# A decoder step on one core: the block inverse widened from 16 to 32, the last output blocks divided 400 and 144, and two products over zeros at the start

## The chip, the cores and the metric

The kernel runs on one core of one Trainium2 chip. Its engines are TensorE (PE, matrix products; PEld is its weight load), VectorE (DVE), ScalarE (ACT), GpSimd (POOL) and SyncE (SP, which issues most of the DMAs). The metric is the time of one execution on the device in microseconds; the time of a kernel is the median of its runs.

## The reference: what is computed

One step of a decoder with one layer, for 512 prompt tokens and 8 sample sequences of 4 tokens, 1024 channels wide. All data is float32. Cut to what matters:

```python
h = rms_norm(x, pre_mix_g)
proj = h @ w_in                               # 1024 x 7424
A = conv_branch(proj[:, :2048])               # GLU, causal conv of width 31, LayerNorm, silu, @ w_conv_out
r, k, v, decay, a, g = ...                    # from proj, with token shift; 16 heads of 64
def step(s, inp):                             # the RWKV-7 recurrence, per head, s is 64 x 64
    r_t, w_t, k_t, v_t, kk_t, a_t = inp
    sk = einsum('bhvk,bhk->bhv', s, kk_t)
    s = s * w_t - sk * (kk_t * a_t) + v_t * k_t
    return s, einsum('bhvk,bhk->bhv', s, r_t)
B = ((group_norm(y) + bonus) * g) @ w_rwkv_out
m = (sigmoid(gA) * A + sigmoid(gB) * B) @ w_out
x = x + rms_norm(m, post_mix_g)
f = square(relu(rms_norm(x, pre_ffn_g) @ w_ff_up)) @ w_ff_down
x = x + rms_norm(f, post_ffn_g)
```

Outputs are the new x and the conv, shift and recurrence states.

## The kernel before

**Layout.** Channels lie on the 128 partitions (8 tiles of 128), tokens on columns: 544 columns, 552 where the 8 shift rows ride along. They are worked in two parts, S1 (276 and 276) or S2 (272 and 272).

**Products.** A weight block of 128 output channels (1024 x 128) is loaded by SP into `raw` (`wraw`, two buffers) and divided into a high part and the remainder, both of type fp32r: `whi` by a cast on ACT or POOL (L140), `wlo` by a subtraction on DVE (L141), two buffers each. The activations are divided likewise (`xh`, `xl`, L173 and L174). A block's product over one part is then 3 matmuls for each of the 8 input tiles (L152 in `part_steps`: whi with xh, whi with xl, wlo with xh). A plain f32 matmul appears in the trace as two records.

**Stages.** x is loaded and normalised (the squares come from ACT at L260, the mean from f32 matmuls with the constant `avg`, L261, one for each of 8 tiles and 2 parts). Then come the blocks of w_in, and between them the recurrence, by pairs of heads (8 pairs, `p`). For a pair the 512 prompt tokens are divided in 8 chunks of 64. Inside a chunk the recurrence is a linear system with a strictly triangular 64 x 64 matrix for each head: its Gram blocks come from PE (L553), are masked into `NQ` and `nd`, and `inverse` replaces the chunk's triangular matrix by the inverse. `chain(p)` then goes through the chunks one after the other (L672 to L687) with `NQ`. Behind it stand `sample` for the sample tokens, the group norm and the output `o`, which goes through DRAM (`o_dr`) to the product with w_rwkv_out. Conv steps (L292, one DVE instruction for each of 31 taps and 8 tiles) fill DVE meanwhile. After the recurrence follow the gate blocks, w_rwkv_out, the LayerNorm of the conv branch (sums L881, variance sum L169), w_conv_out, w_out, and the two halves of the feed-forward part.

**The inverse.** Each chunk's 64 x 64 matrix holds two 32 x 32 diagonal blocks for each of two heads. `nd` with the diagonal blocks is transposed on DVE into `nw` (L588), so that a row of each block lies along the free axis. Fifteen steps of forward substitution (a product, L597, and a subtraction, L599, each on both 16-halves of each block at once) invert the 16 x 16 diagonal blocks in `R`. Two transposes (L602, L604) give `td` and `rd`; copies on ACT (L609) and POOL (L610) set them into the zeroed 64-wide tiles `DT64` and `D64`. What lies outside the 16-blocks, `NQ` under `maskD`, is then brought in by four products, each 8 f32 matmuls, one a chunk (L616): MT = N D, and three times x = D - MT x, the last of which writes `NQ` (L633), the two before it `nw` (L630).

**The end.** The last two blocks of w_ff_down (`last`, 48 matmuls a part) are done part by part: both blocks for the first 272 columns, then both for the second. Their evacuation (L1028) adds the first half's result, `acc_sq` squares it on ACT (L880) and sums it (L881); `rstd` takes the mean over channels on PE (L169) and its inverse root; then for each of 8 tiles two DVE instructions (L1059, L1060) and a store of that tile and part (L1061).

**What sets the order.** A scheduler of the tile framework sets each engine's order from the program, priorities and estimates; the generators' `yield` statements say how the steps of pairs are woven with blocks of projections.

## Time and profile before

| | before |
|---|---|
| median of 3 runs | 1300.46 us (1299.64 to 1304.72) |
| profiled execution, its time | 1299.37 us |
| its span, first to last instruction | 1297.6 us |
| mean granted clock of PE | 0.989 |
| DVE busy | 819.9 us in 1545 instructions |
| ACT busy | 652.0 us in 1563 instructions |
| PE waits for the first product's DT (L609) | 7.8 us, 7 times |

A row of a group reads: line, engine, operation, output from inputs, shape, count, then busy time in us, mean of one in ns, and the idle time of that engine just before them with what ended it. A row of a timeline begins with start and duration in us; the bracket at its end holds the idle time before it. The span is the base of all positions in time. Matmuls follow each other in a pipeline, so what one costs is the distance of starts, not its own duration.

### The profile page before, as it was taken

How to read it: one execution, taken by the hardware profiler on the slowest of the kernel's cores; microseconds unless marked ns; L12 is line 12 of the kernel's file. 1: busy time of each engine (PE TensorE's matmuls, PEld its weight loads, DVE VectorE, ACT ScalarE, POOL GpSimd, SP SyncE). 2: the span in 40 equal slices, each digit the busy share in tenths (PEclk: the TensorE clock that was granted, in tenths of full speed). 3: DMA queues.
4: the chain of work that ended last, by engine and by line, in shares of the span. 5: the costliest groups of instructions: out<-in, count | busy, mean ns of one | idle time of the engine just before them, and what ended most of it. 6: DMA issues, size and time to landing. Idle time of an engine off the chain costs nothing. (4 is left out here: it accounts for less than half of the span.)

```text
span 1297.6 us, 23134 instructions
## 1 busy us (share of the span) xinstructions
PE 1238.4 (95%) x9154; PEld 1162.8 (90%) x9154; DVE 819.9 (63%) x1545; ACT 652.0 (50%) x1563; POOL 198.0 (15%) x286
## 2 busy tenths in 40 slices
PE   7989999999999999999999999999999999999995
PEld 6978888887978888787889999999999999999995
DVE  6889889855888898887677465658432122333345
ACT  7453747575563747538244382356554223554231
POOL 2224232221323233132201100000000000000000
PEclk9989999999999999999999999999999999999998
DMA  6313121120202121131115642361122332232332
GB/s 202 104 33 109 33 82 34 49 69 19 84 33 96 34 81 33 33 95 42 67 48 195 220 167 92 110 209 50 34 82 82 98 86 94 82 97 75 90 98 70
DMA packets 45181, 110.60 MB, mean 85 GB/s; under 512 B 7056, under 2 KB 16528, under 8 KB 45072
## 3 DMA queue, kind: packets, MB, share of 16 engines
q1 hardware_dynamic: 41344, 104.33, 25.6%
q10 hardware_dynamic: 3728, 4.79, 1.1%
q8 instruction: 72, 1.18, 0.4%
q14 instruction: 37, 0.30, 0.1%
HBM read 94.79 MB, written 14.32 MB: 84 GB/s over the span
## 5 line engine op out<-in xcount | busy, mean ns | idle before, releaser
L152 PE MATMUL lin<-xh,whi 128*128 128x272 f32 (+1 forms) x2096 | 616.2, 294 | 4.1 <-DVE r L394 2.0
L152 PE MATMUL lin<-xh,wlo 128*128 128x272 f32 (+1 forms) x2096 | 615.6, 294 | 0.6 <-DVE wlo L141 0.6
L152 PE MATMUL lin<-xl,whi 128*128 128x272 f32 (+1 forms) x2096 | 614.2, 293 | 0.4 <-DVE xl L174 0.2
L152 PEld LDWEIGHTS lin<-xh,whi 128*128 128x128 f32 x2096 | 397.0, 190 | 7.2 <-issue 2.9
L152 PEld LDWEIGHTS lin<-xl,whi 128*128 128x128 f32 x2096 | 396.5, 189 | 3.7 <-issue 1.4
L152 PEld LDWEIGHTS lin<-xh,wlo 128*128 128x128 f32 x2096 | 396.6, 189 | 3.1 <-issue 1.4
L141 DVE TENSOR_TENSOR wlo<-raw,whi 128x1024 fp32r<-128x1024 f32 x131 | 160.7, 1227 | 197.8 <-ACT whi L140 175.7
L292 DVE SCALAR_TENSOR_TENSOR c<-u,cw,c 128x512 f32<-128x512 f32 x240 | 188.0, 783 | 5.7 <-DVE c L292 1.2
L140 ACT CAST whi<-raw 128x1024 fp32r<-128x1024 f32 x76 | 79.7, 1049 | 122.7 <-PE lin L152 119.2
L140 POOL CAST whi<-raw 128x1024 fp32r<-128x1024 f32 x55 | 65.4, 1189 | 319.0 <-PE lin L152 182.9
L152 PE MATMUL lin<-xh,wl 128*128 128x272 f32 x240 | 69.4, 289 | 0.0
L152 PE MATMUL lin<-xl,wh 128*128 128x272 f32 x240 | 69.3, 289 | 0.0
L152 PE MATMUL lin<-xh,wh 128*128 128x272 f32 x240 | 69.2, 288 | 0.0
L1001 DVE TENSOR_TENSOR xl<-ff,xh 128x272 fp32r<-128x272 f32 x64 | 28.3, 442 | 55.9 <-ACT ff L1000 55.9
L687 ACT ACTIVATE SV<-ch,pc 64x64 f32<-64x64 f32 x128 | 39.6, 309 | 19.2 <-PE ch L683 17.8
L228 ACT ACT_TABLE_LOAD x37 | 47.5, 1283 | 1.8 <-PEq L1124 1.2
L152 PEld LDWEIGHTS lin<-xh,wl 128*128 128x128 f32 x240 | 45.2, 188 | 0.1
L152 PEld LDWEIGHTS lin<-xh,wh 128*128 128x128 f32 x240 | 45.2, 188 | 0.1
L152 PEld LDWEIGHTS lin<-xl,wh 128*128 128x128 f32 x240 | 45.1, 188 | 0.1
L681 ACT ACTIVATE SV<-ch 64x64 f32<-64x64 f32 x128 | 27.9, 218 | 33.6 <-PE ch L679 31.6
L760 POOL TENSOR_SCALAR st<-st,epS 128x64 f32<-128x64 f32 x64 | 39.9, 673 | 7.9 <-DVE rt L597 7.9
L998 ACT ACTIVATE ff<-lin 128x272 f32<-128x272 f32 x64 | 25.3, 395 | 29.6 <-PE lin L152 29.5
(274 smaller groups left out, 1830.4 us busy)
## 6 DMA issues: line engine op xcount, KB each, us to landing
raw<-win SPq DMA_DIRECT2D x58, 512.0 KB, 3.7
raw<-wup SPq DMA_DIRECT2D x32, 512.0 KB, 3.6
raw<-wdn SPq DMA_DIRECT2D x32, 512.0 KB, 3.6
g_dr<-g ACTq DMA_DIRECT2D x16, 272.0 KB, 2.9
raw<-wro SPq DMA_DIRECT2D x8, 512.0 KB, 3.7
raw<-wco SPq DMA_DIRECT2D x8, 512.0 KB, 3.6
raw<-wo SPq DMA_DIRECT2D x8, 512.0 KB, 3.6
x<-xT SPq DMA_DIRECT2D x8, 276.0 KB, 4.7
```

The source lines that it names most:

```text
L140: upper(hi, r)
L141: tt(out=lo, in0=r, in1=hi.bitcast(F32), op=SUB)
L152: nc.tensor.matmul(ps, a, b[:, o:o + m], start=k == 0 and i == 0, stop=k == n - 1 and i == 2)
L228: lastact[0] = nc.scalar.preload_act_table_set(name)
L292: stt(out=c[:, 0:T], in0=u[:, t:t + T], scalar=w[:, t:t + 1], in1=c[:, 0:T], op0=MULT, op1=ADD)
L681: nc.scalar.mul(SV[H[i], c, i, :], ch[H[i], 2, B[i]], -1.0)
L687: nc.scalar.mul(SV[H[i], c + 1, i, :], ch[H[i], 1, B[i]], pc[H[i], c:c + 1])
L760: nc.gpsimd.tensor_scalar(st[:, b, :], st[:, b, :], f["epS"][:, b:b + 1], None, MULT)
L998: act(t[:, q], ps, AF.Relu)
L1001: tt(out=lo[:, q], in0=t[:, q], in1=hi[:, q].bitcast(F32), op=SUB)
```

## The change

Three parts. (1) The forward substitution runs 31 steps over whole 32 x 32 blocks instead of 15 over 16 x 16 halves; `maskD` leaves out the whole 32-blocks, and of the four products two remain: MT = N D and one x = D - MT D, which writes `NQ`. (2) The last two down blocks are divided in 400 and 144 columns (S3) instead of two times 272, with the norm, the final operations and the stores. (3) A tile `warm` of 128 x 512 zeros is set on DVE, and two f32 matmuls with `avg` run over it before the statistics of x.

```diff
--- before.py
+++ after.py
@@ -28,6 +28,7 @@
 RMS_EPS, LN_EPS, GN_EPS, KK_EPS = 1e-6, 1e-5, 64e-5, 1e-24
 CDEC = math.exp(-0.5)
 NFP, NFIRST, NPG, UB = 44, 6, 2, 2
+NWARM = 2
 KEPT = 2
 CP, HP, HN = 300, 900, 130
 PUMP, WB, WL, WR = 5, 2, 2, 2
@@ -38,6 +39,7 @@
 
 S1 = ((0, 276), (276, 276))
 S2 = ((0, 272), (272, 272))
+S3 = ((0, 400), (400, 144))
 
 VECS = [("pre_mix_g", 8), ("post_mix_g", 8), ("pre_ffn_g", 8), ("post_ffn_g", 8), ("conv_b", 8),
         ("conv_ln_g", 8), ("conv_ln_b", 8), ("decay_base", 8), ("iclr_base", 8), ("k_k", 8),
@@ -249,6 +251,12 @@
             ready.append(wsplit(raws[-1]))
         avg = p0.tile([128, 128], F32, name="avg")
         nc.vector.memset(avg, 1.0 / D)
+
+        warm = p0.tile([128, 512], F32, name="warm")
+        nc.vector.memset(warm, 0.0)
+        wps = q0.tile([128, 512], F32, name="warmps")
+        for _ in range(NWARM):
+            nc.tensor.matmul(wps, avg, warm, start=True, stop=True)
         rs, rt = (p0.tile([128, N1], F32, name=n) for n in ("rs", "rt"))
         hfs = [p0.tile([128, N1], F32, name=f"hf{k}") for k in range(KT)]
         with start:
@@ -353,16 +361,13 @@
         nc.gpsimd.memset(maskD, 0.0)
         maskP = p1.tile([128, 2, 64], F32, name="maskP")
         nc.gpsimd.memset(maskP, 0.0)
-        first16 = p1.tile([128, 1], F32, name="first16")
-        nc.vector.tensor_reduce(out=first16, in_=con("bmask")[:, 0:4], op=ADD, axis=mybir.AxisListType.X)
         for i in range(2):
             q = slice(64 * i, 64 * i + 64)
             nc.scalar.copy(maskD[q, :, i, :], mask[q].rearrange("p (a t) -> p a t", a=2))
             nc.scalar.copy(maskP[64 * i:64 * i + 32, i, :], maskS[64 * i:64 * i + 32])
             for g in range(2):
                 r, o = slice(64 * i + 32 * g, 64 * i + 32 * g + 32), 32 * g
-                nc.gpsimd.memset(maskD[r, 0, i, o:o + 16], 0.0)
-                nc.scalar.copy(maskD[r, 0, i, o + 16:o + 32], first16[r].to_broadcast([32, 16]))
+                nc.gpsimd.memset(maskD[r, 0, i, o:o + 32], 0.0)
         zar = p1.tile([128, NB, 16], F32, name="zar")
         nc.gpsimd.memset(zar, 0.0)
         zbk = p1.tile([128, 2, 64], F32, name="zbk")
@@ -588,14 +593,12 @@
             nc.vector.transpose(nt.rearrange("p s t -> p t s"),
                                 nd.rearrange("p c t -> p t c").unsqueeze(3).to_broadcast([128, 32, NC, 4]))
             yield DVE
-            half = lambda t, d, o, n: bass.AP(tensor=t.tensor, offset=t.offset + o, ap=[t.ap[0], [d, 2], *n])
-            for s in range(15):
-                nj, n = s // 4 + 1, 15 - s
-                tmp = p1.tile([128, 64], F32, name="rt")
-                tv = tmp[:, 0:2 * nj * n].rearrange("p (a j t) -> p a j t", a=2, j=nj)
-                rv = half(R, 144, s + 1, [[32, nj], [1, n]])
-                tt(out=tv, in0=half(R, 144, s, [[32, nj], [0, n]]),
-                   in1=half(nt, 528, 33 * s + 1, [[0, nj], [1, n]]), op=MULT)
+            for s in range(31):
+                nj, n = s // 4 + 1, 31 - s
+                tv = p1.tile([128, 80], F32, name="rt")[:, 0:nj * n].rearrange("p (j t) -> p j t", j=nj)
+                rv = R[:, 0:nj, s + 1:32]
+                tt(out=tv, in0=R[:, 0:nj, s:s + 1].to_broadcast([128, nj, n]),
+                   in1=nt[:, s:s + 1, s + 1:32].to_broadcast([128, nj, n]), op=MULT)
                 tt(out=rv, in0=rv, in1=tv, op=SUB)
                 yield DVE
             td = p1.tile([128, NC, 32], F32, name="td", tag="nd")
@@ -623,16 +626,10 @@
                 for i in range(2):
                     nc.scalar.copy(MT[H[i], :, i, :], ps[H[i]])
             yield from product(lambda c: NQ[:, c, 0], DT64, to_m)
-            x = D64
-            for it in range(3):
-                def to_x(ps):
-                    if it < 2:
-                        tt(out=xn, in0=D64, in1=ps, op=SUB)
-                    else:
-                        for i in range(2):
-                            tt(out=NQ[H[i], :, 0, i, :], in0=D64[H[i]], in1=ps[H[i]], op=SUB)
-                yield from product(lambda c: MT[:, c], x, to_x)
-                x = xn
+            def to_x(ps):
+                for i in range(2):
+                    tt(out=NQ[H[i], :, 0, i, :], in0=D64[H[i]], in1=ps[H[i]], op=SUB)
+            yield from product(lambda c: MT[:, c], D64, to_x)
 
         def tokens(p):
 
@@ -880,9 +877,9 @@
             act(sq[:, q], src[:, q], AF.Square)
             tt(out=acc[:, q], in0=acc[:, q], in1=sq[:, q], op=ADD)
 
-    def rstd(rs, acc, eps, s):
+    def rstd(rs, acc, eps, s, split=S2):
         t = temp("rt")
-        f32sum(con("avg"), acc, S2[s:s + 1],
+        f32sum(con("avg"), acc, split[s:s + 1],
                lambda _, ps, o, m: rsqrt(rs[:, o:o + m], ps, eps, t[:, o:o + m]), **aux)
 
     def rstd_sum(rs, src, eps, s):
@@ -1049,11 +1046,11 @@
                 linear(w, fhl, S2, down(j))
 
     last = [(j, wload(wdn[j, 2], pg) + wload(wdn[j, 3], pg)) for j in (KT - 2, KT - 1)]
-    for s in range(2):
-        q = HALF[s]
+    for s, (o, m) in enumerate(S3):
+        q = slice(o, o + m)
         for j, w in last:
-            part_mm(w, fhl, s, *S2[s], down(j), pl2, "lin")
-        rstd(rs, acc, rms_eps, s)
+            part_mm(w, fhl, s, o, m, down(j), pl2, "lin")
+        rstd(rs, acc, rms_eps, s, S3)
         for j in range(KT):
             f = part[j][:, q]
             stt(out=f, in0=f, scalar=nvec("post_ffn_g", j), in1=rs[:, q], op0=MULT, op1=MULT)
```

In the changed kernel L154 is L152 of before, L143 is L141, L171 is L169, L300 is L292, L600 and L602 are the substitution's L597 and L599, L878 is L881, L1025 is L1028, L1056 and L1057 are L1059 and L1060.

DVE in the inverse of pair 0, between the transposes into `nw` and `td`. Before (`rt` and `R` are the substitution, `c` a conv step):

```order
L597 TENSOR_TENSOR rt<-R,nw 128x36
L292 SCALAR_TENSOR_TENSOR c<-u,cw,c 128x512
L599 TENSOR_TENSOR R<-R,rt 128x2x2x9
L289 TENSOR_SCALAR c<-u,cw,vt 128x512
L597 TENSOR_TENSOR rt<-R,nw 128x32
L292 SCALAR_TENSOR_TENSOR c<-u,cw,c 128x512
L599 TENSOR_TENSOR R<-R,rt 128x2x2x8
```

And now, where `wlo` is a weight's remainder and `k` a part of the next pair's projections:

```order
L600 TENSOR_TENSOR rt<-R,nw 128x63
L300 SCALAR_TENSOR_TENSOR c<-u,cw,c 128x512
L602 TENSOR_TENSOR R<-R,rt 128x3x21
L143 TENSOR_TENSOR wlo<-raw,whi 128x1024
L600 TENSOR_TENSOR rt<-R,nw 128x60
L392 SCALAR_TENSOR_TENSOR k<-lin,omu,k 128x276
L602 TENSOR_TENSOR R<-R,rt 128x3x20
L300 SCALAR_TENSOR_TENSOR c<-u,cw,c 128x512
L600 TENSOR_TENSOR rt<-R,nw 128x76
L300 SCALAR_TENSOR_TENSOR c<-u,cw,c 128x512
L602 TENSOR_TENSOR R<-R,rt 128x4x19
```

An operation of the substitution still alternates with one other instruction, but there are 62 instead of 30 of them: 127 instructions stand between the two transposes, 61 before.

PE behind the recurrence, where `aux` from `acc` is the variance sum of the conv LayerNorm. Before, it stands inside a gate block (`lin_7677`):

```order
L152 MATMUL lin_7677<-xh_91,wlo_7623 128x272
L152 MATMUL lin_7677<-xh_93,whi_7622 128x272
L152 MATMUL lin_7677<-xl_94,whi_7622 128x272
L152 MATMUL lin_7677<-xh_93,wlo_7623 128x272
L169 MATMUL aux_8550<-acc_8517,cs_74 128x272
L169 MATMUL aux_8559<-acc_8517,cs_74 128x272
L152 MATMUL lin_7677<-xh_95,whi_7622 128x272
L152 MATMUL lin_7677<-xl_96,whi_7622 128x272
```

Now it stands among the first products with w_rwkv_out (`lin_8224`, `lin_8250`, `lin_8285`; `xh_8168` to `xl_8199` are parts of `o`):

```order
L154 MATMUL lin_8250<-xl_8193,whi_8220 128x272
L154 MATMUL lin_8250<-xh_8192,wlo_8221 128x272
L154 MATMUL lin_8285<-xh_8168,wlo_8282 128x272
L154 MATMUL lin_8285<-xh_8174,whi_8281 128x272
L154 MATMUL lin_8285<-xl_8175,whi_8281 128x272
L154 MATMUL lin_8285<-xh_8174,wlo_8282 128x272
L154 MATMUL lin_8224<-xh_8198,whi_8220 128x272
L154 MATMUL lin_8250<-xh_8198,whi_8220 128x272
L171 MATMUL aux_8773<-acc_8740,cs_74 128x272
L171 MATMUL aux_8782<-acc_8740,cs_74 128x272
L154 MATMUL lin_8224<-xl_8199,whi_8220 128x272
```

The gate blocks that stood between have moved ahead, into the recurrence: from the last pair's output (`yt`) to this sum there are now 170 projection matmuls.

DVE at the end, where the first part's final operations give way to the second part's evacuation. Before:

```order
L1059 SCALAR_TENSOR_TENSOR f<-f,nvt,frs 128x272 x2
L1060 TENSOR_TENSOR f<-f,m 128x272 x2
L1028 TENSOR_TENSOR f<-lin,f 128x272
L881 TENSOR_TENSOR facc<-facc,sq 128x272
L1028 TENSOR_TENSOR f<-lin,f 128x272
L881 TENSOR_TENSOR facc<-facc,sq 128x272
L111 SCALAR_TENSOR_TENSOR rt<-aux,epst,rt 128x272
L112 SCALAR_TENSOR_TENSOR frs<-rt,frs 128x272
```

And now:

```order
L1056 SCALAR_TENSOR_TENSOR f<-f,nvt,frs 128x400 x2
L1057 TENSOR_TENSOR f<-f,m 128x400 x2
L1025 TENSOR_TENSOR f<-lin,f 128x144
L878 TENSOR_TENSOR facc<-facc,sq 128x144
L1025 TENSOR_TENSOR f<-lin,f 128x144
L878 TENSOR_TENSOR facc<-facc,sq 128x144
L113 SCALAR_TENSOR_TENSOR rt<-aux,epst,rt 128x144
L114 SCALAR_TENSOR_TENSOR frs<-rt,frs 128x144
```

All sixteen operations of the first part stand ahead of the second part's first evacuation, as before; they are 400 columns wide, and the second part's 144.

## The prediction

> **What bounds the kernel now.** I read the engines' busy time first, then windows by stage, then the waits of the engine that is busiest, then single instructions where the change works.
>
> ```profile
> PE 1238.4 (95%) x9154; PEld 1162.8 (90%) x9154; DVE 819.9 (63%) x1545; ACT 652.0 (50%) x1563; POOL 198.0 (15%) x286
> 60.00:700.00 640.00, 607.36 (x4251) 540.12 (x4252) 513.87 (x1011) 356.92 (x978) 175.49 (x244) 0.99 0.20 62
> 700.00:1260.00 560.00, 554.90 (x4378) 552.12 (x4377) 244.21 (x395) 256.90 (x486) 7.76 (x5) 1.00 0.34 106
> 1280.00:1297.60 17.60, 4.51 (x33) 3.87 (x31) 10.78 (x28) 2.21 (x5) 0.00 (x0) 0.74 0.29 102
> ```
>
> In a window's row stand its length, the busy time of PE, PEld, DVE, ACT and POOL with instructions, the granted clock, and the DMA share and GB/s. PE is the bound to 1280: 607 of 640 us in the recurrence stage, 555 of 560 in the projections behind it. DVE has 126 us spare in the recurrence, but it is a chain there, so its spare time says little about when one result is ready. In the last 17.6 us DVE is the bound. Less PE work in the recurrence therefore shortens the time one for one, as long as nothing makes PE wait.
>
> **Products removed.** Two of four products a pair go.
>
> ```profile
> 131.73 1.90 PE L616 MATMUL pb<-nw,MT 128*128 128x64 f32 x16
> L616 PE MATMUL pb<-nw,MT 128*128 128x64 f32 x256 | 31.9, 279 | 0.0
> L630 DVE TENSOR_TENSOR nw<-D,pb 128x512 f32<-128x512 f32 x16 | 11.0, 688 | 19.2 <-PE pb L616 19.2
> PE pb L616 <- ACT DT L609: 7.8, 7, 1.7
> ```
>
> The second row is exactly what goes: 256 records, two for each f32 matmul, 32 a pair. Their 279 ns overlap; what one takes from its neighbour is its spacing, (1.90 − 0.28)/15 = 0.108 us from the first row. 256 × 0.108 = **−27.7 us** of PE. The 19.2 us idle in the third row are DVE's, not PE's, so nothing is added for them; DVE loses the 11.0 us.
>
> **The longer substitution.** 62 instructions on DVE replace 30 in each pair, and each follows the one before it through R, with other work between.
>
> ```profile
> 91.10 1.97 PE L553 MATMUL pb<-LR,BK 128*128 128x256 f32 x8
> 96.75 2.05 DVE L588 STREAM_TRANSPOSE nw<-nd 128x1024 f32<-128x1024 f32 x1
> 110.31 0.19 DVE L597 TENSOR_TENSOR rt<-R,nw 128x42 f32<-128x42 f32 x1
> 110.42 0.74 DVE L292 SCALAR_TENSOR_TENSOR c<-u,cw,c 128x512 f32<-128x512 f32 x1
> 111.09 0.19 DVE L599 TENSOR_TENSOR R<-R,rt 128x42 f32<-128x42 f32 x1
> 123.15 0.41 DVE L602 STREAM_TRANSPOSE td<-R 128x256 f32<-128x256 f32 x1
> 125.30 2.00 PE L616 MATMUL pb<-DT,NQ 128*128 128x64 f32 x16 [0.39 <-ACT DT L609]
> L597 DVE TENSOR_TENSOR rt<-R,nw 128x24 f32<-128x24 f32 (+10 forms) x120 | 24.7, 206 | 0.8
> L599 DVE TENSOR_TENSOR R<-R,rt 128x24 f32<-128x24 f32 (+10 forms) x120 | 30.0, 250 | 0.8
> ```
>
> A small operation holds a slot of 0.11 us (110.31 to 110.42), a conv step 0.67 (110.42 to 111.09). As capacity this is cheap: 256 more operations at 0.11 to 0.23 us (the mean of the last two rows) are 28 to 59 us, less the 11.0, so DVE comes to 531 to 562 us of what would be some 612. The price is in the order. In pair 0 DVE has 61 instructions between the two transposes before, 30 of them the substitution's, and they take 123.15 − (96.75 + 2.05) = 24.35 us, 0.40 each. The new order has 127 there, 62 and 65 others: 127 × 0.40 = 50.8 us, or 24.35 + 32 × 0.11 + 34 × 0.67 = 50.7 if all others were conv steps, about 47 since they are also weight remainders and rates. So the first product is later by 22.6 to 26.4 us. On PE that time is filled by work drawn forward: between the last Gram matmul (91.10) and the first product stand 193 projection matmuls before and 339 now. 146 × 0.125 us (the spacing of two starts, below) = 18.3, and 43 more short f32 records of the tokens and sample steps at 0.108 to 0.26 are some 5 to 6: 24 us. The two nearly balance. Today PE waits for DT in 7 pairs of 8, 7.8 us in all, so the margin is nothing now and nothing then. Bounds: −7.8 (the waits vanish) to 8 × 2.2 = +17 (DVE takes 26.4, PE's cover 24.2). I take a little over the middle, **+5**: 0.6 us a pair. What else moves: the chain over chunks of a pair now runs under the next pair's projections with less other PE work between its links; I cost it at nothing, since the work displaced from it is the work that now covers the inverse. If that cover is gone, it shows as PE waiting for SV.
>
> **The end of the recurrence.** Work drawn forward is missing at the end. Before, sixteen groups of 24 gate projections follow the last pair's output, 48 us; now five and a half do, some 17 us, then the products with w_rwkv_out, whose inputs pass through DRAM.
>
> ```profile
> 689.63 0.29 PE L152 MATMUL yt<-xh,llo 128*128 128x272 f32 x1
> 689.96 0.44 DVE L790 TENSOR_TENSOR t<-yt,t 128x272 f32<-128x272 f32 x1
> 704.24 1.68 PE L169 MATMUL aux<-acc,cs 128*128 128x272 f32 x4 [1.84 <-issue]
> 719.73 0.71 DVE L881 TENSOR_TENSOR acc<-acc,sq 128x544 f32<-128x544 f32 x1
> 1258.55 0.29 PE L152 MATMUL lin<-xl,whi 128*128 128x272 f32 x1
> ...
> 1259.93 0.29 PE L152 MATMUL lin<-xh,wh 128*128 128x272 f32 x1
> ```
>
> The last two rows are eleven spacings apart: 1.38/11 = 0.125 us for 272 columns. From the last output operation (ends 690.40) to the last sum of squares of the conv LayerNorm (ends 720.44) DVE, with the DMAs it waits for, needs 30.0 us. In the new order PE has 170 projection matmuls and one f32 sum from the last yt matmul to the variance sum that waits there: 170 × 0.125 + 1 = 22.3 us, begun 0.6 before DVE's 30.0. PE lacks 30.0 + 0.6 − 22.3 = 8.3, and 1.8 of it (the row at 704.24) it waits there already: about **+6.5**. Bounds: 0, since part of DVE's 30 us is waiting for DMAs and casts that may come sooner, and +12, since PE can also wait for the splits of the o tiles.
>
> **The tail.** 400 columns come first, then 144.
>
> ```profile
> 130.59 0.68 PE L447 MATMUL aux<-k,cs 128*128 128x272 f32 x2
> 1271.02 0.44 DVE L1028 TENSOR_TENSOR f<-lin,f 128x272 f32<-128x272 f32 x1 [4.57 <-PE lin L152]
> 1281.88 0.43 DVE L1028 TENSOR_TENSOR f<-lin,f 128x272 f32<-128x272 f32 x1
> 1282.80 0.44 DVE L881 TENSOR_TENSOR facc<-facc,sq 128x272 f32<-128x272 f32 x1 [0.50 <-ACT sq L880]
> 1283.82 0.44 DVE L1028 TENSOR_TENSOR f<-lin,f 128x272 f32<-128x272 f32 x1 [0.58 <-PE lin L152]
> 1293.90 0.78 DVE L1060 TENSOR_TENSOR f<-f,m 128x272 f32<-128x272 f32 x2
> L1060 DVE TENSOR_TENSOR f<-f,m 128x272 f32<-128x272 f32 x16 | 6.3, 432 | 0.0
> L935 DVE TENSOR_TENSOR c<-c,rs 128x544 f32<-128x544 f32 x8 | 5.2, 717 | 0.0
> L880 ACT ACTIVATE sq<-f 128x272 f32<-128x272 f32 x14 | 6.0, 429 | 41.1 <-DVE f L1028 41.1
> L880 ACT ACTIVATE sq<-c 128x544 f32<-128x544 f32 x7 | 4.4, 657 | 2.0 <-DVE c L929 2.0
> ```
>
> From a part's last f to the end of its sixteen operations DVE takes 10.86 us (1271.02 to 1281.88, and 1283.82 to 1294.68). The last four rows give the price of a column: (717 − 432)/272 = 1.05 ns on DVE, (657 − 429)/272 = 0.84 on ACT. 128 columns more or less are 20 × 0.134 + 4 × 0.107 + 0.2 = 3.3 us on that chain. PE's first part takes 96 × (0.125 × 400/272 = 0.184) = 17.6 instead of 12.0, so its last f starts at 1276.6; sixteen wide operations end 14.2 later, at 1290.8. The second part's PE work, 96 × 0.066 to 0.11 us (by proportion, or the spacing of the 64-column records), is done by then. DVE then does its first f, square and facc (1282.80 + 0.44 − 1281.88 = 1.36, 1.0 at 144 columns) and a chain of 10.86 − 3.3 = 7.5: end 1299.3 against 1294.68, **+4.6**. A wide first part pays where PE is what the end waits for; here it is DVE.
>
> **The warm-up.** Two products over zeros run on PE while it would wait for x.
>
> ```profile
> 4.00:7.00 3.00, 2.52 (x6) 1.91 (x7) 1.02 (x2) 2.21 (x6) 0.93 (x1) 1.00 1.04 382
> 7.64 0.43 ACT L260 ACTIVATE sq<-x 128x276 f32<-128x276 f32 x1 [0.49 <-PE ss L261]
> 8.56 0.43 ACT L260 ACTIVATE sq<-x 128x276 f32<-128x276 f32 x1 [0.49 <-PE ss L261]
> 8.90 1.03 ACT L140 CAST whi<-raw 128x1024 fp32r<-128x1024 f32 x1
> 10.43 0.49 ACT L235 ACTIVATE rs<-ss,epst 128x276 f32<-128x276 f32 x1 [0.50 <-PE ss L261]
> ```
>
> Each sum over 276 columns takes 0.92 us until 8.56 (two squares apart), against 0.68 for such a pair in the row at 130.59, the filling of its pipeline included: slow, though the granted clock of the first row reads 1.00. The statistic is ready at 10.43, and rs follows at once. But ACT has the weight cast (ends 9.93) ahead of rs, and in the new order two more squares: an earlier statistic finds ACT busy. I cost it **0**, −1 to +1. The Trainium skill, "TensorE: Matmul & The Clock Gate", Part 1, says that PE starts at half clock and that some 3.4 us of sustained activity release it, in a free-running window; by that rule the warm products would bring the statistics forward by some 2 us and the time with them. The trace's slow sums agree with the half clock, the cast at 8.90 speaks against the gain.
>
> **The sum.** −27.7 + 5 + 6.5 + 4.6 + 0 = −11.6. The profiled execution took 1299.37 us, 1.1 below the median of the runs: 1287.8, or 1288.9 by the median; I say 1288. Half a per cent, about what a measurement tells from no change, is 6.5 us: 1294 and 1307 are the bounds.
>
> **The rivals.**
> - The gain is kept: DVE's sequence does not delay PE and the end of the recurrence is filled. For it: 126 us of DVE are free. Against it: PE waits for DT already. −27.7 + 0 + 0 + 4.6, and some 1 less: 1276.
> - 144 columns are slow. No fp32r row in the trace is under 272 columns wide; f32 needs two records for 272 columns, 0.68 us less a filling of 0.29 − 0.125, so 0.26 each. At f32 pace a 144-column matmul is 2 × 0.26 × 144/272 = 0.28 us, and 96 of them 26 us: PE ends the second part at 1276.6 + 27, the end is 8 behind, +17 for the tail in place of 4.6: 1300, no change. It binds as soon as one takes over 14.2/96 = 0.148 us.
> - Slower: DVE's substitution outruns PE. If one of its rows takes 0.43 us, not 0.40, as when ACT and POOL hold up the other work among them, 127 rows are 54.6, PE waits 3.5 us more a pair than in the sum: +28 for eight: about 1310 with the rest. It decides from 2.4 us more a pair (19 us, to 1307). Against it: pairs behind the first have much of the conv work gone.
> - The warm-up gains by the rule above, 2 us: 1285.5.
>
> **How the numbers follow.** Forecast 0.44 (alone 1281 to 1293), gain kept 0.17, slow 144 columns 0.17, slower 0.14, warm-up 0.08. The range 1276 to 1302 takes in the first, the second, the third and the fifth to their middle and leaves out the slower case. Faster: 0.42 of the forecast, 0.17, 0.02 of the slow columns and 0.08: 0.69. Slower: half of its rival, 0.07. Same: the rest, 0.24.
>
> **What would show it.** The group of products should fall from 512 records to 256. The wait of PE for DT should be 5 to 20 us in all, and the rows between the transposes 45 to 55 us long. A PE wait of 4 to 10 us for acc or an o tile should stand at the conv LayerNorm's sums. In the tail PE's 144-column matmuls should be spaced under 0.148 us, with DVE's wide operations at 0.55 to 0.6 us, and rs should start no earlier than 10. I am wrong if PE idles in the recurrence for SV or DT by tens of us, or if the 144-column rows are spaced 0.25 us.

## The result, and the profile after

The changed kernel takes 1324.66 us (median of four executions) against 1302.59 us before: a ratio of 1.0173, 95% interval 1.0148 to 1.0198. It is slower by 1.7%, where 1288 was forecast. One of the four executions, the profiled one, ran the whole time with PE at 0.55 of its clock (1918 us) and is left aside; the other three lie between 1323.62 and 1325.64. All rows of the changed kernel below come from a second measurement of the same file (e1_after_again: 1323.97 us, ratio 1.0182, 1.0160 to 1.0204), whose profiled execution took 1322.2 us with a span of 1320.4.

Busy time of the engines, and windows as in the prediction:

```profile
PE 1238.5 (94%) x8902; PEld 1152.5 (87%) x8902; DVE 851.9 (65%) x1785; ACT 651.3 (49%) x1559; POOL 188.5 (14%) x286
60.00:700.00 640.00, 593.02 (x4027) 521.54 (x4026) 542.74 (x1243) 347.42 (x951) 171.06 (x246) 0.97 0.20 61
700.00:1260.00 560.00, 543.95 (x4200) 537.15 (x4199) 237.55 (x387) 259.19 (x501) 3.12 (x3) 0.98 0.33 103
```

PE has 252 records fewer than before and is busy for as long, 1238.5 us against 1238.4. It is idle for 1320.4 − 1238.5 = 81.9 us, before for 59.2. So slower work on PE has eaten the 27.7 us, and 22.7 us of idle time come on top. The slower work is in part the clock: it is lower in both windows (0.97 and 0.98, before 0.99 and 1.00), and ahead of the tail the trace's clock records show 0.5 in 13 stretches, 54.6 us in all, before in 5 stretches, 20.5 us. PE is busy in them for 48.4 us, before for 19.0; if work goes half as fast there, 15 us are lost. The other 13 us or so, the wider tail and the two products over zeros among them, were not divided up.

The waits of PE, longest total first:

```profile
PE aux L452 <- DVE k L535: 7.7, 3, 3.9
PE lin L154 <- DVE xl L176: 5.5, 4, 3.8
PE lin L154 <- DVE r L399: 5.2, 2, 3.1
PE aux L171 <- DVE facc L878: 4.6, 2, 3.5
PE lin L154 <- DVE wlo L143: 4.1, 2, 3.6
PE pb L619 <- ACT DT L612: 4.0, 2, 3.5
```

The wait that the prediction watched, for DT, has shrunk from 7.8 to 4.0 us. The waits that have grown are on other work of DVE: k and r of the next pair (L535, L399), and at the end of the recurrence the split of `o` (xl, L176).

The timeline of pair 0, DVE's rows first, then PE's: the transposes into `nw` and `td`, the write of `NQ`, the next pair's `nw`; the first product, the first chunk of the chain that needs `NQ`, the next pair's first Gram matmul.

```profile
95.58 2.04 DVE L593 STREAM_TRANSPOSE nw<-nd 128x1024 f32<-128x1024 f32 x1
150.27 0.44 DVE L605 STREAM_TRANSPOSE td<-R 128x256 f32<-128x256 f32 x1
157.93 1.41 DVE L631 TENSOR_TENSOR NQ<-D,pb 64x512 f32<-64x512 f32 x2 [0.82 <-PE pb L619]
177.51 1.96 DVE L593 STREAM_TRANSPOSE nw<-nd 128x1024 f32<-128x1024 f32 x1
152.44 0.32 PE L619 MATMUL pb<-DT,NQ 128*128 128x64 f32 x1
159.98 0.38 PE L676 MATMUL ch<-xs,NQ 128*128 128x128 f32 x2
160.20 0.38 PE L558 MATMUL pb<-LR,BK 128*128 128x256 f32 x1
```

Read in order of time, one thing hangs on the other. The transpose into `nw` takes 2.0 us, the substitution from its end to `td` 52.6, then it is 2.2 more to the first product, 6.9 for the two products until `NQ` is written, 0.6 to the chain; the next Gram matmul starts 0.2 behind it, and 17.3 later the next `nw`. That is 81.9 us for a pair. Before, in the same place, with PE's first chunk of the chain and first Gram matmuls behind it:

```profile
136.96 1.38 DVE L633 TENSOR_TENSOR NQ<-D,pb 64x512 f32<-64x512 f32 x2
138.85 0.38 PE L679 MATMUL ch<-xs,NQ 128*128 128x128 f32 x2
147.79 0.67 PE L553 MATMUL pb<-LR,BK 128*128 128x256 f32 x2
166.59 1.95 DVE L588 STREAM_TRANSPOSE nw<-nd 128x1024 f32<-128x1024 f32 x1
```

The write of `NQ` ended at 138.3 and the pair took 69.8 us: 24.4 for the substitution and 13.0 for four products. The changed kernel gives up 28 us in the one and gets 6 back in the other, 22 us net, but its period is only 12.1 us longer. The rest was slack: before, the next `nw` came 28.3 us behind the end of `NQ`, now 18.2, since the Gram matmuls no longer start 9 us behind the chain but 0.2.

Pair 0 is typical of the path and not of the loss. In six of the seven pairs that have a successor, the next `nw` now follows `NQ` by 17.7 to 18.8 us (22.4 in pair 2, whose substitution takes 23.7 us); before, it was 28.3 to 45.6. So the path from `nw` to `nw` has become tight nearly everywhere, where each pair had 10 us of slack or more. The seven periods together grew by less than seven times 12: from the first `nw` to the last it is 540.4 us, before 525.8. The last pair pays once more. It has no successor; gate blocks run beside it on PE, which is busy for 35.4 of the 37.7 us of its substitution:

```profile
622.56 2.04 DVE L588 STREAM_TRANSPOSE nw<-nd 128x1024 f32<-128x1024 f32 x1
637.68 0.45 DVE L602 STREAM_TRANSPOSE td<-R 128x256 f32<-128x256 f32 x1
635.97 1.96 DVE L593 STREAM_TRANSPOSE nw<-nd 128x1024 f32<-128x1024 f32 x1
675.64 0.45 DVE L605 STREAM_TRANSPOSE td<-R 128x256 f32<-128x256 f32 x1
```

Pair 7 starts 13.4 us late (622.56 and 635.97, before and after) and its substitution ends 38.0 us late. The span ends 22.8 us late: some of the work that stood behind the recurrence has been done by then.

### The profile page after: what moved, and what is told of

Same layout as the page of the kernel before. It is cut to its first block, busy times and chain, and to the rows that moved or that the text cites. A ratio compares the mean times of both kernels' runs of the same rounds, so it can differ in the third digit from the quotient of the medians.

```text
span 1916.6 us, 22885 instructions
## 1 busy us (share of the span) xinstructions
PE 1894.9 (99%) x8902; PEld 1770.9 (92%) x8902; DVE 840.8 (44%) x1785; ACT 654.0 (34%) x1559; POOL 174.7 (9%) x286
## 3 DMA queue, kind: packets, MB, share of 16 engines
q1 hardware_dynamic: 41344, 104.33, 17.3%
## 4 chain that ended last, share of the span: by engine, by line
PE 97%; DVE 2%; ACT 1%; issue 0%; DVEq 0%; ACTq 0%
PE lin L154 74%; PE pb L558 3%; PE pb L619 2%; PE yt L452 1%; PE ch L676 1%; PE ch L680 1%; PE ch L671 1%; PE yt L681 1%; PE yt L673 1%; PE ch L669 1%; PE aux L452 1%; PE aux L723 1%; PE aux L154 1%; PE ch L648 1%; PE ss L269 1%; PE aux L754 1%
## 5 line engine op out<-in xcount | busy, mean ns | idle before, releaser
L154 PE MATMUL lin<-xh,wlo 128*128 128x272 f32 (+1 forms) x2096 | 849.4, 406 | 2.2 <-DVE wlo L143 2.2
L154 PE MATMUL lin<-xh,whi 128*128 128x272 f32 (+1 forms) x2096 | 845.8, 405 | 5.5 <-DVE g L910 2.1
L154 PE MATMUL lin<-xl,whi 128*128 128x272 f32 (+1 forms) x2096 | 846.7, 404 | 1.5 <-DVE xl L176 1.5
L154 PEld LDWEIGHTS lin<-xh,whi 128*128 128x128 f32 x2096 | 503.8, 241 | 28.5 <-issue 6.3
L154 PEld LDWEIGHTS lin<-xh,wlo 128*128 128x128 f32 x2096 | 504.1, 241 | 21.7 <-issue 5.8
L154 PEld LDWEIGHTS lin<-xl,whi 128*128 128x128 f32 x2096 | 502.7, 240 | 21.0 <-issue 5.5
L143 DVE TENSOR_TENSOR wlo<-raw,whi 128x1024 fp32r<-128x1024 f32 x131 | 161.3, 1231 | 373.3 <-ACT whi L142 297.1
L300 DVE SCALAR_TENSOR_TENSOR c<-u,cw,c 128x512 f32<-128x512 f32 x240 | 178.6, 745 | 9.8 <-issue 8.6
L154 PE MATMUL lin<-xh,wl 128*128 128x272 f32 (+2 forms) x240 | 99.3, 414 | 0.0
L154 PE MATMUL lin<-xl,wh 128*128 128x272 f32 (+2 forms) x240 | 98.6, 411 | 0.0
L154 PE MATMUL lin<-xh,wh 128*128 128x272 f32 (+2 forms) x240 | 98.0, 409 | 0.0
L998 DVE TENSOR_TENSOR xl<-ff,xh 128x272 fp32r<-128x272 f32 x64 | 28.3, 442 | 121.6 <-ACT ff L997 121.6
L154 PEld LDWEIGHTS lin<-xh,wh 128*128 128x128 f32 x240 | 58.3, 243 | 4.2 <-issue 0.7
L154 PEld LDWEIGHTS lin<-xh,wl 128*128 128x128 f32 x240 | 58.0, 242 | 4.1 <-issue 0.7
L154 PEld LDWEIGHTS lin<-xl,wh 128*128 128x128 f32 x240 | 58.2, 242 | 3.6 <-issue 0.2
L558 PE MATMUL pb<-LR,BK 128*128 128x256 f32 x128 | 61.1, 579 | 0.0
L600 DVE TENSOR_TENSOR rt<-R,nw 128x60 f32<-128x60 f32 (+24 forms) x248 | 59.6, 240 | 3.0 <-issue 1.1
L602 DVE TENSOR_TENSOR R<-R,rt 128x60 f32<-128x60 f32 (+24 forms) x248 | 59.2, 239 | 2.0
```

The costliest lines, as they stand in the source:

```text
L143: tt(out=lo, in0=r, in1=hi.bitcast(F32), op=SUB)
L154: nc.tensor.matmul(ps, a, b[:, o:o + m], start=k == 0 and i == 0, stop=k == n - 1 and i == 2)
L300: stt(out=c[:, 0:T], in0=u[:, t:t + T], scalar=w[:, t:t + 1], in1=c[:, 0:T], op0=MULT, op1=ADD)
L558: nc.tensor.matmul(ps[:, c], BK[:, 4 * g + c], LR[:, 4 * g + c], start=True, stop=True)
L600: tt(out=tv, in0=R[:, 0:nj, s:s + 1].to_broadcast([128, nj, n]), in1=nt[:, s:s + 1, s + 1:32].to_broadcast([128, nj, n]), op=MULT)
L602: tt(out=rv, in0=rv, in1=tv, op=SUB)
```

## The experiments

Theory A and its rivals B, C, P, T, L and S are named in the expectations as they were formed. All ratios are to the kernel before on the same chip, and microseconds from a ratio take that kernel as 1303. The edits are cut to the lines that matter.

**Which part costs.** The changed kernel again (above), and each part alone.

> The changed kernel once more, to see its profile at full clock. About 1324 us again. Theory A (the longer substitution keeps PE waiting): PE idles in the recurrence for DT or SV, 35 us or more over the eight pairs beyond what it waited before, which eats the 27.7 us of removed products and some 20 more; the tail costs about 5. Theory B (the narrow matmuls): 144-column matmuls are spaced 0.25 us or more at full clock and the tail alone has grown by 17 us or more. Theory C (the clock): PE waits no more than before, but matmuls of 272 columns are spaced about 1.5% wider for some stretch, as the mean clock of 0.974 against 0.989 hints.

Measured: 1323.97 us, with the rows above. The 35 us of A at DT or SV are not there: the wait for DT has shrunk, and from 60 to 700 us PE is idle for 640 − 593.0 = 47.0 us in all, before for 32.6. C's condition, that PE waits no more than before, does not hold either.

The kernel without the warm products and with `S3 = S2`, so that only the inverse is changed:

```diff
-S3 = ((0, 400), (400, 144))
+S3 = S2
-        for _ in range(NWARM):
-            nc.tensor.matmul(wps, avg, warm, start=True, stop=True)
```

> The changed kernel without the warm products and with the last blocks divided in 272 and 272: only the inverse is changed. Theory A: 1316 to 1322 us, nearly the whole loss. Theory B: 1290 to 1300, faster than before. Theory C by the warm products: as B; theory C by the denser PE work itself: about 1318 with a clock of 0.975.

Measured: 1321.46 us, ratio 1.0158 (1.0137 to 1.0178). Nearly the whole loss is in the inverse, as A had it. C by denser work comes near too (its profile has a clock of 0.975), but PE is not denser: it is busy for 1234.5 of 1318.5 us, before for 1238.4 of 1297.6.

The kernel before with the tail of the changed one:

```diff
+S3 = ((0, 400), (400, 144))
-    for s in range(2):
-        q = HALF[s]
+    for s, (o, m) in enumerate(S3):
+        q = slice(o, o + m)
```

> The kernel before with the last two blocks divided in 400 and 144 columns, nothing else. Theories A and C: 1303 to 1307, the 4.6 us of the prediction's tail. Theory B: 1317 or more, with 144-column matmuls spaced 0.25 us.

Measured: 1308.26 us, 1.0038 (1.0015 to 1.0061), about 5 us (2 to 8). In its timeline, DVE's last f of the first part, the first f of the second and the last operation; then spacings of PE at 400 and 144 columns:

```profile
1282.93 0.57 DVE L1029 TENSOR_TENSOR f<-lin,f 128x400 f32<-128x400 f32 x1 [6.95 <-PE lin L153]
1297.08 0.30 DVE L1029 TENSOR_TENSOR f<-lin,f 128x144 f32<-128x144 f32 x1
1305.35 0.53 DVE L1061 TENSOR_TENSOR f<-f,m 128x144 f32<-128x144 f32 x2
1274.70 0.35 PE L153 MATMUL lin<-xl,wh 128*128 128x400 f32 x1
...
1276.16 0.35 PE L153 MATMUL lin<-xh,wh 128*128 128x400 f32 x1
1290.78 0.28 PE L153 MATMUL lin<-xl,wh 128*128 128x144 f32 x1
1290.89 0.28 PE L153 MATMUL lin<-xh,wl 128*128 128x144 f32 x1
```

The wide chain takes 1297.08 − 1282.93 = 14.15 us, worked out as 14.2; eight starts at 400 columns are 1.46 us apart, 0.183 each, worked out as 0.184; 144 columns are spaced 0.11, so B falls.

The kernel before with the warm products:

```diff
+        nc.vector.memset(warm, 0.0)
+        for _ in range(NWARM):
+            nc.tensor.matmul(wps, avg, warm, start=True, stop=True)
```

> The kernel before with the two products over zeros, nothing else. Theories A and B: 1299 to 1303, no change. Theory C by the warm products: 1315 or more and a mean clock of 0.975. The clock gate's rule: the sums of squares are spaced under 0.7 us some 2 us earlier and the time falls by 1 to 2 us.

Measured: 1304.82 us, 1.0007 (0.9988 to 1.0026): no change that can be measured. The sums of the first part before, and then here with what follows on ACT:

```profile
4.47 5.92 PE L261 MATMUL ss<-sq,avg 128*128 128x276 f32 x16 [4.47 <-ACT sq L260]
5.08 3.88 PE L268 MATMUL ss<-sq,avg 128*128 128x276 f32 x16
8.96 0.75 ACT L267 ACTIVATE sq<-x 128x276 f32<-128x276 f32 x2
9.62 0.47 ACT L236 ACTIVATE rs<-ss,epst 128x276 f32<-128x276 f32 x1
```

The sums of the first part now take 3.88 us, before 5.92, and are done at 8.96 instead of 10.39; the trace's clock records begin, at full clock, at 4.8 us instead of 8.4. That is what the Trainium skill, "TensorE: Matmul & The Clock Gate", Part 1, has for PE that was kept busy first. But rs starts at 9.62, behind the cast and two squares on ACT, only 0.8 us sooner, and of 0.8 us nothing shows in a total that is known to some 2 us.

**What in the inverse costs.** Theories A and P were put to a square: 15 or 31 steps, with two or four products.

```diff
-            for it in range(3):
+            for it in range(1):
-                    if it < 2:
+                    if it < 0:
```

> The kernel before with two products a pair instead of four, the substitution left at 15 steps over 16-blocks (the result leaves out the later corrections of the inverse). Theory A (DVE paces the recurrence once the substitution is long, PE before): this kernel is still paced by PE and gains most of the 27.7 us: 1272 to 1282. Theory P (time is PE's instructions plus its waits, and each part adds its own): the same, 1273 to 1278. Theory T (the products were hidden by waits anyway): 1295 to 1303.

Measured: 1285.80 us, 0.9867 (0.9830 to 0.9904): −17 us, less than the 20 to 30 of A and P and more than T's 0 to 8. The first of its waits:

```profile
PE pb L616 <- ACT DT L609: 10.4, 8, 2.0
```

In all 8 pairs PE comes to the first product too early, before in 7. Its profiled execution (1288.61 us) has PE idle for 65.4 us, before 59.2, and 51.2 us at half clock ahead of the tail, before 20.5: if PE loses half of that, 15 us, the two are more than what is missing from 27.7.

The other corner is the changed inverse with the loop of three put back:

> The inverse with 31 steps and all four products (the added two correct nothing any more, M squared being zero); no warm products, columns 272 and 272. Theory A: the removed products were worth little beside the long substitution, since DVE sets the pace there: 1321 to 1335. Theory P: the kernel with two products plus 27.7 us, 1346 to 1352.

Measured: 1363.53 us, 1.0461 (1.0427 to 1.0495). Neither fits. Beside the long substitution two products are worth (1.0461 − 1.0158) × 1303 = 39 us, more than their 27.7 us on PE and more than the 17 they are worth beside the short one. The rows of pair 0 show where they come out:

```profile
97.00 2.04 DVE L587 STREAM_TRANSPOSE nw<-nd 128x1024 f32<-128x1024 f32 x1
151.36 0.44 DVE L599 STREAM_TRANSPOSE td<-R 128x256 f32<-128x256 f32 x1
165.63 1.38 DVE L630 TENSOR_TENSOR NQ<-D,pb 64x512 f32<-64x512 f32 x2
185.78 1.96 DVE L587 STREAM_TRANSPOSE nw<-nd 128x1024 f32<-128x1024 f32 x1
```

From `td` to the end of `NQ` it is 15.7 us, in the changed kernel 9.1, and the next `nw` comes 6.9 us later for the pair's start (88.8 us after the last, against 81.9). What is put into the pair's path comes out in its period, as there is no slack left: in all seven pairs that have a successor the next `nw` follows `NQ` by 17.7 to 18.8 us. This is theory S: the path is closed from `nw` to the next `nw`. On PE the 39 us show as the 27.7 of the products' own work, 5 us more of idle time (88.9 us against 84.0 with two products) and 20.5 us more at half clock ahead of the tail (78.5 against 58.0), of which half is lost. So P, with the clock's loss added, comes out near the measured time as well; A, in which the amount of work on DVE sets the pace, has no such price for products.

**Amount or path.** Half the conv steps left out (the convolution has 16 of its 31 taps) relieves DVE, in the changed inverse and in the kernel before:

```diff
-        for t in range(1, CW):
+        for t in range(1, CW, 2):
```

> Only the inverse changed (31 steps, two products), and 15 of the 30 conv steps of each tile left out (the convolution has 16 taps), which takes 120 x 0.67 = 80 us from DVE. Theory A: PE's waits for DVE in the recurrence and behind it go, and with them the half-clock stretches: 1268 to 1285, below the next kernel. Theory L (the chain of 62 dependent operations itself is too long, whatever DVE has beside it): 1305 or more.

> The kernel before with the same 15 conv steps a tile left out, as the control of the kernel above. Theory A: PE sets the pace already, so little is won: 1288 to 1300, and the kernel above is 10 to 27 us faster than this one. Theory L: 1288 to 1300 too, and the kernel above is slower than this one.

Measured: 1293.69 us (0.9935, 0.9910 to 0.9961) and 1310.55 us (1.0060, 1.0038 to 1.0083). The changed inverse gains 28 us and is now the faster of the two, though not below 1285 as A had it; the kernel before gains nothing and even loses 0.6%, which A had not expected. In the first of them, pair 1's substitution:

```profile
177.59 1.97 DVE L587 STREAM_TRANSPOSE nw<-nd 128x1024 f32<-128x1024 f32 x1
205.62 0.43 DVE L599 STREAM_TRANSPOSE td<-R 128x256 f32<-128x256 f32 x1
```

26 us with all 62 operations. Three of the eight pairs take 26 to 27 us, the others 34 to 52, where conv steps or other instructions still stand between. So the chain itself is not too long (L falls); what makes it 53 us is the conv step or other instruction that stands behind each of its rows. A and S both allow this. The next two runs were to part them, one with the substitution on POOL, one with free work on DVE:

```diff
-                tt(out=tv, in0=R[:, 0:nj, s:s + 1].to_broadcast([128, nj, n]),
+                nc.gpsimd.tensor_tensor(out=tv, in0=R[:, 0:nj, s:s + 1].to_broadcast([128, nj, n]),
-                tt(out=rv, in0=rv, in1=tv, op=SUB)
+                nc.gpsimd.tensor_tensor(out=rv, in0=rv, in1=tv, op=SUB)
```

> The changed inverse alone (31 steps, two products), with the 62 instructions of the substitution on POOL instead of DVE; the conv steps that stood between them on DVE no longer do. Theory S (a pair's dependent chain, substitution then products then the chain over chunks, closes a loop whose length is the period of a pair; it was 82 us with the long substitution, 53 of it between the transposes): if an operation on POOL takes 0.5 to 0.7 us, the substitution takes 31 to 43 us, the period falls to 60 to 72 us, PE sets the pace again and the time is 1275 to 1295. Theory A (DVE's amount of work): DVE loses 55 us a run, the same 1275 to 1290. If POOL is slower than 0.8 us an operation, S says 1315 or more and A still 1290 or less.

Measured: 1448.23 us, 1.1123 (1.1095 to 1.1152), which neither expected.

```profile
L594 POOL TENSOR_TENSOR rt<-R,nw 128x60 f32<-128x60 f32 (+24 forms) x248 | 83.9, 338 | 107.3 <-DVE zn L733 86.6 <-DVE nw L587 4.0
PE pb L613 <- ACT DT L606: 150.4, 8, 20.9
```

POOL is quick enough: 338 ns an operation, and `td` follows `nw` by 28 to 37 us. But PE waits for DT 150 us in 8 times: in pair 0, 152 projection matmuls stand between the last Gram matmul and the first product, in the kernel with only the inverse changed 327, and PE stands still for 19 us a pair. S had the substitution's length right (31 to 43 us) and the rest wrong: a pair takes 82 to 102 us, not 60 to 72. So the length of the path does not give the time without the order in which PE gets its work. A misses too, and the run does not tell A from S.

```diff
+                for i in range(2):
+                    dm = p1.tile([128, 16], F32, name="dm")
+                    tt(out=dm, in0=con("eye")[:, 0:16], in1=con("eye")[:, 16:32], op=MULT)
```

> The kernel before with two more small DVE instructions in each of the 15 steps (240 in all, 16 columns, about 0.11 us each, 26 us of DVE), on a tile that nobody reads: as many as the change adds, but outside of the dependent chain. Theory A (DVE's amount of work paces): slower by 15 to 40 us, 1317 to 1340. Theory S (only what lengthens the pair's loop counts): within 6 us of before, with the time between the transposes still 13 to 25 us.

Measured: 1325.05 us, 1.0170 (1.0148 to 1.0192): what A expects, and a miss for S. But the added rows are not where they were meant to be. They wait for nothing, and the scheduler drew them forward: the first runs at 31.8 us, the last at 393.6, and only 50 of the 240 stand between two transposes. The row of a window shows their time on DVE and their count ahead of pair 0; behind it stands the same wait on PE, before and here:

```profile
31.70:66.20 34.50, 10.71 (x48) 0.98 0.31 93
74.80 0.36 PE L152 MATMUL lin<-xh,whi 128*128 128x272 f32 x1 [2.03 <-DVE r L394]
82.53 0.36 PE L152 MATMUL lin<-xh,whi 128*128 128x272 f32 x1 [1.75 <-DVE r L394]
```

48 added rows hold DVE for 10.7 us there, and PE is 7.7 us late before the first pair's inverse begins. So this run is no clean test, and another was made: the kernel with two products and 15 steps, with 32 operations a pair that wait for each other, 60 columns wide, placed behind the transposes.

```diff
+            dm = p1.tile([128, 64], F32, name="rt")[:, 0:60]
+            tt(out=dm, in0=con("eye")[:, 0:60], in1=con("eye")[:, 64:124], op=MULT)
+            for i in range(31):
+                tt(out=dm, in0=dm, in1=con("eye")[:, 0:60], op=MULT)
             def product(lhsT, rhs, out):
```

> The kernel with two products and 15 steps (1286 us), and 32 more DVE instructions a pair of 60 columns, each waiting for the one before it, on a tile that nobody reads, placed behind the transposes of the inverse: as many instructions on DVE as the long substitution has, taken one with another, but no longer ahead of the products. Theory S (the pair's path substitution, products, chain over chunks closes the loop): 1283 to 1296, near the kernel without them. Theory A (DVE's amount of work): 1315 to 1325, as the kernel with 31 steps and two products.

Measured: 1280.60 us, 0.9835 (0.9803 to 0.9867), a little below S's range. The added rows, the recurrence's window here and then in the kernel with only the inverse changed, and pair 0 here:

```profile
L616 DVE TENSOR_TENSOR rt<-rt,cs 128x60 f32<-128x60 f32 x248 | 67.8, 273 | 0.9
60.00:700.00 640.00, 601.12 (x4128) 533.42 (x4126) 555.29 (x1276) 365.89 (x997) 179.59 (x247) 0.98 0.20 66
60.00:700.00 640.00, 591.90 (x3985) 520.31 (x3985) 543.15 (x1245) 345.05 (x943) 171.59 (x246) 0.97 0.19 60
98.76 2.04 DVE L588 STREAM_TRANSPOSE nw<-nd 128x1024 f32<-128x1024 f32 x1
125.16 0.41 DVE L602 STREAM_TRANSPOSE td<-R 128x256 f32<-128x256 f32 x1
```

DVE is busier in the recurrence than with the long substitution (555.3 us against 543.2, and 1276 instructions against 1245), and the kernel is (1.0158 − 0.9835) × 1303 = 42 us faster. A falls. The operations are the same kind in the same number; what differs is that no product waits for them, and `td` comes 24.4 us behind `nw`. Between `NQ` and the next `nw` there are again 31 us or more, in every pair that has a successor.

**The clock.** More idle time on PE comes, in the main, with more time at half clock. From the profiled executions (PE's idle time, and its stretches at half clock ahead of the tail, in us):

| kernel | span | idle | half clock |
|---|---|---|---|
| before | 1297.6 | 59.2 | 20.5 |
| changed | 1320.4 | 81.9 | 54.6 |
| only the inverse changed | 1318.5 | 84.0 | 58.0 |
| 15 steps, two products | 1286.9 | 65.4 | 51.2 |
| 31 steps, four products | 1363.3 | 88.9 | 78.5 |
| 240 added rows | 1324.9 | 73.5 | 51.2 |
| 15 steps, two products, 32 added rows a pair | 1279.5 | 63.9 | 30.7 |

The stretches follow waits. One in the kernel with only the inverse changed:

```profile
435.97 1.17 PE L446 MATMUL aux<-k,cs 128*128 128x272 f32 x2 [3.15 <-DVE k L529]
438.56 0.43 PE L154 MATMUL lin<-xl,whi 128*128 128x272 f32 x1
438.79 0.43 PE L154 MATMUL lin<-xh,wlo 128*128 128x272 f32 x1
436.04:439.45 3.41, 2.36 (x7) 1.57 (x8) 3.41 (x9) 2.13 (x6) 2.68 (x5) 0.50 0.00 0
439.45:442.87 3.42, 3.42 (x15) 3.19 (x15) 2.91 (x10) 0.00 (x0) 0.00 (x0) 0.50 0.13 45
```

After 3.15 us without work the matmuls are spaced 0.23 us instead of 0.125, for 6.83 us, twice 3.41, and the clock of both windows reads 0.50. The Trainium skill, "TensorE: Matmul & The Clock Gate", Part 1, has a window of 3413 ns, and the trace agrees with it. Shorter waits can do it too: in the kernel before, the waits ahead of the five stretches are of 1.1 to 2.7 us. Theory C, that the warm products or the denser work themselves lower the clock, is not needed: the warm products alone changed nothing, and of the two windows shown for e11_free_chain the one in which PE is busier (601.1 us against 591.9) has the higher clock. Work that does nothing was put ahead of the wait for DT, in the kernel before:

```diff
+                if rhs is DT64:
+                    for _ in range(2):
+                        nc.tensor.matmul(ps[:, 0:4, :].rearrange("p c t -> p (c t)"), con("avg"),
+                                         td.rearrange("p c t -> p (c t)"), start=True, stop=True)
```

> The kernel before with two f32 matmuls of 256 columns ahead of each pair's first product, on td, whose result is overwritten: PE does something useless where it otherwise waits for DT. If the half-clock stretches of the records (five before the tail, 20.5 us in all) come from those waits and cost about half their length, fewer of them should stand in the recurrence and the time be 2 to 6 us less; if not, it is the cost of the useless work, 0 to +5 us.

Measured: 1310.55 us, 1.0065 (1.0043 to 1.0088): slower by some 8 us, more than the useless work was to cost. The half-clock stretches are as long as before, 20.5 us in all, with PE busy in 18 of them, before in 19; so the run says nothing on what they cost.

## Why the prediction was wrong

**The step that failed is "The longer substitution", +5.** The instruction counts in it were right, and nearly so the durations: 127 rows were put at 47 to 50.8 us, and they took 52.6, 0.41 a row, between the 0.40 of the forecast and the 0.43 of the slower rival. Right too was that PE would wait little for DT: 4.0 us, even under the 5 to 20 that were named as a sign. What was wrong is the conclusion that a first product which comes 28 us later costs what PE waits for it. I checked one meeting point, DT, and let the rest of the pair move along "at nothing". But the next pair's Gram matmuls stand right behind the start of this pair's chain (0.2 us in pair 0), so once the slack of 10 us or more is used up, a later `NQ` is a later `nw` for the next pair, and a later last pair. The delay comes up elsewhere: as waits for k, r and xl, and as half-clock stretches behind them. From the square, 31 steps instead of 15 with two products cost (1.0158 − 0.9867) × 1303 = 38 us, where +5 and +6.5 stood for them. The spans of the two profiled executions differ by 31.6 us: 18.6 are idle time of PE, 2 or 3 the half clock, and the rest is slower work on PE that was not traced.

**"The products removed", −27.7,** was mis-sized: −17 us by themselves (e5_two_products). The removed PE work is there, but PE waits 10.4 us for DT in that kernel, before 7.8, is idle for 6 us more in all, and its profiled execution has 31 us more at half clock. The term counted PE's own work alone. How the missing 10 us of the median divide between idle time and clock was not settled, since that execution took 2.8 us more than the median.

**"The end of the recurrence", +6.5,** was right in kind: PE waits there, for xl, 3.8 us at once, and from 700 to 1260 us it is idle for 16.1 us, before for 5.1. That is 11 us more, near the upper bound of 12. It is a part of the 38 us and cannot be separated from them. Its sum, from the last output on, left out that the last pair itself ends late: `td` of pair 7 is 38 us behind.

**"The tail", +4.6,** was right, size and mechanism: about 5 us, with 14.15 us for the wide chain. **"The warm-up", 0,** was right, for the reason given: ACT has other work first, though rs started at 9.62 in the kernel with the warm products alone and 9.94 in the changed one, a little ahead of the 10 that was named as a sign. The 1.00 that the prediction read as the granted clock from 4 to 7 us is no measurement: the clock records of that trace begin at 8.4 us.

With the terms as measured, −17 + 38 + 5 + 1 = +27 us; the changed kernel shows +22 to +24. The first two add up to the 21 us of e2_inverse_only by the way they were taken, so the sum checks only that inverse, tail and warm-up add up.

Of the rivals, the one on the other side named the place (the substitution outruns PE) and missed the way: it looked for a PE wait at DT that grows by 3.5 us a pair. Its time has a slip: 28 us more than in the sum is 1316, not 1310. The gain that is kept fell with the result. Narrow matmuls fell (0.11 us a spacing). The gain by the warm-up fell: the statistic came 1.4 us earlier, rs 0.8, and no change of the total could be measured. The first reason that I formed afterwards, the amount of work on DVE, fell as well.

What stays open: how 240 idle rows, most of them outside the inverse, cost 22 us (e10_free_rows); they show as 14 us more of idle time on PE and 31 us more at half clock, but why the order brings those was not traced. Open too is what sets the period when the path is short and PE waits all the same (e9_steps_on_pool). Three kernels that should have cost nothing moved by 0.6% to 1.7% when the order around the edit changed, so a difference of that size between two orders proves no mechanism here. The effects that carry the explanation, 38 and 42 us, are larger. Whether the Gram matmuls follow the chain because of PE's order or because they share the buffer `pb` with the products wasn't tried. The one kernel faster than both, with two products on 16-blocks, leaves out corrections of the inverse; one that keeps them all and beats the kernel before was not found.

## What to carry to other kernels

Before a dependent chain is lengthened, follow it round to its own start in the next iteration and add it up; the period less that sum is the slack, here 10 us in pair 0, and what goes in beyond it comes out, however idle the engines are. An engine's spare time tells what it can take off the path, not on it: in a queue where the order places one filler, mostly of 0.67 us, behind each short link, 32 more links cost 28 us. And work removed from the busiest engine need not be worth its own length: two products of 27.7 us on PE were worth 17 us beside the short substitution and 39 beside the long one, where they lay on the path.

## What the runs showed of the hardware

- fp32r matmuls of 144 columns start every 0.11 us, of 272 every 0.125 and of 400 every 0.183: 144 columns take 88% of the time of 272.
- Waits on PE are followed by 3.41 us, or a multiple, at half clock. Counted in 13 profiles (all but the one at 0.55; from 60 us after the start to 30 us before the end), all 34 waits of 3 us or more had such a stretch begin in them or within 3.41 us of their end, 43 of 46 waits of 2 to 3 us, and 38 of 95 of 1 to 2 us. At spacings of 0.23 instead of 0.125 us a stretch of 3.41 us costs some 1.6 us.
- A substitution's operation takes 338 ns on POOL and 252 to 262 on DVE (by records).
